# Two attention generators stepped at more ticks, a drain that becomes a poll, and a scale moved from VectorE to GpSimd

## Chip, cores and metric

The kernel runs on one core of one Trainium2 chip. The metric is device time in microseconds: 1560.05 us is the median of 3 runs (1555.44 to 1561.1). The profiled execution took 1560.56 us.

## What is computed

Two transformer blocks run one after the other on 512 tokens of width 1024, in float32. Each mixes tokens in several ways and ends in a feed-forward network. Cut to what matters here:

```python
def first_block(x, mem, ...):
    h = rmsnorm(x, g_pre_mix)
    cb, cc, cv, q, k, v, qm, ga, gb, gc = split(h @ w_in)
    y_a = (cb * causal_dwconv(cc * cv)) @ w_conv_out
    y_b = moba_attention(q, k, v, rel_bias) @ w_attn_out        # 8 heads of 64
    y_c = memory_attention(qm, rmsnorm(mem)) @ w_mem_out        # 4 heads of 128, 256 keys
    merged = sigmoid(ga) * y_a + sigmoid(gb) * y_b + sigmoid(gc) * y_c
    x = x + rmsnorm(merged @ w_out)
    u = causal_dwconv(rmsnorm(x) @ w_up)
    return x + rmsnorm((gelu(a) * g) @ w_down)                  # a, g = halves of u

def second_block(x, mem, ...):
    hq, hf, hi, hg, sq, sk, sv, iq, ik, iw, mq = split_in(rmsnorm(x) @ w_in)
    o_hg = hgrn2_mix(hq, hf, hi, hg)        # gated linear recurrence, chunks of 64
    o_sa = dsa_mix(sq, sk, sv, iq, ik, iw)  # attention on 128 keys picked by an index score
    o_mem = mem_mix(mq, rmsnorm(mem))       # 4 heads of 64, 256 keys
    x = x + concat(o_hg, o_sa, o_mem) @ w_out
    return x + (silu(a) * b) @ w_ffn_out    # a, b = halves of rmsnorm(x) @ w_ffn_in
```

## The kernel before

**GEMMs.** A float32 weight tile of 128 x 1024 is split into a high part (a cast on ScalarE, `wh`) and a low part (a subtraction on VectorE, `wl`), both in a 32-bit format that TensorE takes in one pass. A product is three passes: high by high, high by low, low by high (`passes`). Most jobs are 24 matmuls of 512 columns. Three pairs of buffers hold split tiles, and a tile is split two jobs ahead of its use.

**The order.** The program writes the order of every engine itself. `Program.job` lists the GEMM work. Beside it run generators, started by name with `Program.start`: each step of one issues some matmuls, reductions or copies of an attention head. After each few matmuls comes a tick. At a tick (`Program.tick`) each generator's credit grows by its rate, and one with a credit of 1 is advanced by a step, if the planner's `Clock` finds what it waits for ready (`clear`). Generators of rank 0 go first. `Program.drain(name)` closes a stage: it advances *all* generators until the named one has ended, and no GEMM is issued meanwhile.

**Block 1.** Convolution, then the gates: `gate(br, m, use)` is one job of 24 matmuls (`w_in_gate`, a tanh on ScalarE) and one of 12 (the branch's output weight). The generator `moba` runs the eight heads of local attention as four pairs (`moba_pair`, `causal_pair`): per pair four steps of scores with a reduction on VectorE (`tensor_tensor_reduce`) and an exponential on ScalarE, then row scalings on ScalarE, 20 transposes, copies out of PSUM, and 8 products. It is drained before the memory's queries are projected. `memT` norms and transposes the memory beside it. The generator `mem` runs the four heads of memory attention (`mem_heads`) beside the gates of the second branch and is drained before those of the third. `splits` splits block 2's weights ahead of time: a fetch on ScalarE's queue, a cast on ScalarE, a subtraction on VectorE, two writes on ScalarE's queue to DRAM, part after part. Its first twelve parts are drained after the third branch; then `w_out` follows.

**Block 2, the mixing stage.** `idx` makes the index scores and selects keys with VectorE (`top_keys`). `mem2` is memory attention, `fin_mq` (named `finm`) makes its queries. `hgrn_levels` computes the recurrence's products inside a chunk group by ten levels (m = 256 down to 0) for each half of the heads, two levels in flight. A level (`Level.steps`) is: subtractions on GpSimd, exponentials on ScalarE, a multiplication by the gated query (`scale`), and products on TensorE with a copy or a masked copy into an accumulator. `hgrn_tail(j)` makes the output of half j: products, a norm (ScalarE square, VectorE reduction, a power on GpSimd, VectorE multiplication) and 8 transposes. `sa` runs the selected attention as two pairs. The last GEMM, `w_out_2`, takes its first weight tile after `mem2`, the second after a drain of `sa`, the third after a drain of `tail0` and `tail1`.

In the rows that follow `p` is a PSUM bank, `s` a 128 x 1024 slot, `t` a scratch tile, `m` a column of statistics. All instructions carry line 96, that of the recording wrapper.

Of the kernel before, what the change touches and what calls it, by code (L numbers as in the profile page):

```python
# [13 lines left out]
ALU = mybir.AluOpType  # L14
# [187 lines left out]
def chain(*gens):  # L202
    def f():
        for g in gens:
            yield from g()
    return f


def body(tc, ctx, io):
    nc = tc.nc  # L210
    clock = Clock()
    v_, a_, g_, pe, sync = (Engine(e, n, clock) for e, n in (
        (nc.vector, "DVE"), (nc.scalar, "ACT"), (nc.gpsimd, "POOL"), (nc.tensor, "PE"), (nc.sync, "SP")))
# [27 lines left out]
    def passes(out, sh, sl, mh, ml, start, stop):  # L241
        mm(out, sh, mh, start=start, stop=False)
        mm(out, sh, ml, start=False, stop=False)
        mm(out, sl, mh, start=False, stop=stop)
# [50 lines left out]
    pr = Program(load, split, clock)  # L295
# [174 lines left out]
    def gemm_N(srcs, x, use, nt=NT):  # L470

        outs = []
        n = len(srcs)

        def f(kp):
            def g(w):
                if kp == 0:
                    outs.extend(bank() for _ in range(nt))
                if kp == n - 1:
                    for t in range(nt):  # L480
                        for kk in range(2):
                            tile_pass(outs[t], x(), 2 * kp + kk, t, w, kk, False, kk == 1)
                        use(t, outs[t])
                        if t < nt - 1:
                            yield
                    outs.clear()
                    return
                for kk in range(2):
                    i = 2 * kp + kk
                    for t in range(nt):  # L490
                        tile_pass(outs[t], x(), i, t, w, kk, i == 0, False)
                        if (kk * nt + t) % 2 and kk * nt + t < 2 * nt - 1:
                            yield
            return g
        for kp in range(n):
            pr.job(f(kp), [srcs[kp]])
# [128 lines left out]
    def toeplitz(hd):  # L625
        t = tmp()
        base = rdram[hd]
        for r in range(0, P, RB):
            a_.dma_start(t[r:r + RB, :], bass.AP(tensor=base.tensor, offset=base.offset + P - 1 - r, ap=[[639, RB], [1, 512]]))
        return t  # L630
# [20 lines left out]
    def stacked(out, q, kh, kl):  # L651
        mm(out, q, kh, start=True, stop=False)
        mm(out, q, kl, start=False, stop=True)
# [203 lines left out]
    def moba_pair(c):  # L857
        def g():
            while ("kl", c) not in qk:
                yield  # L860
            tz = [toeplitz(2 * c), toeplitz(2 * c + 1)]
            yield from causal_pair(
                lambda s: tuple(qk[n, c][:, s, :] for n in ("q", "kh", "kl")),
                lambda s, j: vN[j // 2][:, j % 2, (2 * c + s) * 64:(2 * c + s) * 64 + 64],
                lambda s, i: tz[s][:, 384 - P * i:512], lambda ps: oT.put(c, ps), extra=tz)
            yield
        return g
# [1 line left out]
    head_chunks([io["w_in_qk"][i] for i in (0, 4, 1, 5)], H, [use_q(0), use_k(0), use_q(1), use_k(1)],  # L869
                {(0, 1): small_consts, (0, 3): lambda: late_T(2), (1, 0): lambda: late_T(3), (1, 1): bias_rows})  # L870
    gemm_N([io["w_in_v"][j] for j in range(4)], H, use_v)
    pr.start("moba", chain(*(moba_pair(c) for c in range(4))), 0.35)
    cj = {c: conv_jobs(c) for c in range(4)}
    for c in range(4):
        for n, f in enumerate(cj[c]):
# [55 lines left out]
    def mem_head(hd):  # L931
        def g():
            def score(t, o):
                c = slice(t * P, (t + 1) * P)
                passes(o, qm.hi(hd)[:, c], qm.lo(hd)[:, c], mkv["kh"][:, hd, :], mkv["kl"][:, hd, :], True, True)
            yield from mem_heads([(score, lambda j: tuple(mkv[n][:, j, hd * P:(hd + 1) * P] for n in ("vh", "vl")), 0, P)],
                                 P ** -0.5, lambda ps: omT.put(hd, ps), parts=True,
                                 inputs=(qm.c[hd], mkv["kh"], mkv["kl"], mkv["vh"], mkv["vl"]))
        return g
# [10 lines left out]
    for c in range(4):  # L950
        chunk(io["w_mk"][c], lambda: memT, use_mk(c), cols=(0, 256))
    gemm_N([io["w_mv"][j] for j in range(4)], lambda: memT, use_mv, nt=2)
    pr.start("mem", chain(*(mem_head(hd) for hd in range(4))), 0.5)
    M = {n: [Parts(io[n][j]) for j in range(io[n].shape[0])]
         for n in ("w_hf", "w_hq", "w_iq", "w_mqsv", "w_sqk", "w_hi", "w_hg")}
    M["w_ikw"] = [Parts(io["w_ikw"])]
# [120 lines left out]
    def use_iq(c):  # L1077
        def f(ps):
            iq[c] = slot([P, 2, 512], F32R)
            stack_q([iq[c][:, s, :] for s in range(2)], ps)  # L1080
        return f
# [187 lines left out]

    def mem2_pair(c):  # L1270
        def g():
            hs = []
            for s in range(2):
                hd = 2 * c + s

                def score(t, o, hd=hd):
                    stacked(o, m2["q"].head(hd)[:, t * P:(t + 1) * P], m2["kh"].head(hd), m2["kl"].head(hd))
                hs.append((score, lambda j, hd=hd: m2["v"][:, j, hd * 64:(hd + 1) * 64], 64 * s, 64))
            yield from mem_heads(hs, 1.0, lambda ps: mixed.put(6 + c, ps),
                                 inputs=(m2["q"].head(2 * c), m2["q"].head(2 * c + 1), m2["kh"].all, m2["kl"].all))  # L1280
        return g
# [80 lines left out]
    class Level:  # L1362
# [39 lines left out]
                a_.activation(ke, ke, AF.Exp)  # L1402

        def scale(self):
            v_.tensor_tensor(out=self.qo, in0=self.qo, in1=self.blk(self.sq)[:, :, 1, :], op=ALU.mult)

        def steps(self):
            if self.m:
# [184 lines left out]
    def mixing():  # L1593
        next_head((late2, swap2), M["w_ikw"] + M["w_iq"][:3], [use_ikw, use_iq(0), use_iq(1), use_iq(2)], park)
        pr.start("idx", chain(sel0, index_weights, *(index_scores(c) for c in range(4)), top_keys(3),
                              top_keys(2), top_keys(1)))
        pr.start("hgrn", hgrn_levels)
        chunk(M["w_iq"][3], H, use_iq(3))
        gemm_N(M["w_mqsv"], H, use_mqsv)
        pr.start("finm", fin_mq, rank=0)  # L1600
        pr.ctl(load_kv2)
        for c in (0, 1):
            chunk(M["w_hf"][c], H, use_hf(c))
        for c in (0, 1):
            chunk(M["w_hq"][c], H, use_hq(c))
            if c == 0:
                pr.drain("finm")
                pr.start("mem2", chain(mem2_pair(0), mem2_pair(1)), rank=0)
        pr.start("gates0", gates(0), rank=0)
        gemm_N(M["w_sqk"], H, use_sqk)  # L1610
        pr.start("fin", fin_sqk, rank=0)
        for c in (2, 3):
            chunk(M["w_hf"][c], H, use_hf(c))
        for c in (2, 3):
            chunk(M["w_hq"][c], H, use_hq(c))
        pr.start("gates1", gates(1), rank=0)
        gemm_N(M["w_hi"], H, use_hi)
        pr.start("tail0", hgrn_tail(0))
        pr.start("sa", chain(sa_pair(0), sa_pair(1)))
        pr.start("tail1", hgrn_tail(1))  # L1620
        for c in range(4):
            chunk(M["w_hg"][c], H, use_hg(c))

    mixing()


# [175 lines left out]
```

## Time and profile before

| | us |
|---|---|
| median of 3 runs | 1560.05 |
| profiled execution | 1560.56 |
| its span, first to last instruction | 1558.7 |
| TensorE busy | 1511.8 (97%) |
| VectorE busy | 784.9 (50%) |
| ScalarE busy | 595.0 (38%) |
| GpSimd busy | 174.0 (11%) |

The profile is of one execution. Busy time of TensorE includes time at the lower clock level; a granted clock of 1.00 is 2.4 GHz and 0.50 is 1.2 GHz. In a timeline, a row's bracket is the engine's idle time before it and who released it. Releasers are inferred; where the engine named had long been done, it was another.

### The profile page before, as it was taken

The numbers are of one execution on the slowest core, as the hardware profiler recorded it, in microseconds if no ns is written. First come the engines' busy times: TensorE is split into PE (matmuls) and PEld (weight loads), VectorE is DVE, ScalarE is ACT, GpSimd is POOL, SyncE is SP. The second block draws the span as 40 slices with busy tenths as digits, with TensorE's granted clock in tenths as the row PEclk, the third lists the DMA queues.
The fourth block names the chain that finished last, engine by engine and source line by source line (L and its number), as shares of the span: only waits on it lengthen the run. The fifth ranks groups of instructions, "written<-read, shape, count | busy, mean of one in ns | idle before, by whom it ended". The sixth has DMA issues, their size and how long they took to land.

```text
span 1558.7 us, 20413 instructions
## 1 busy us (share of the span) xinstructions
PE 1511.8 (97%) x8059; PEld 1259.4 (81%) x8059; DVE 784.9 (50%) x1186; ACT 595.0 (38%) x1025; POOL 174.0 (11%) x290
## 2 busy tenths in 40 slices
PE   8999998998999999999999999999779999999999
PEld 7888887886888888888888888787568888888887
DVE  5355443465465676666522448885445333333231
ACT  5354354444453544434322334464524222222120
POOL 1000000022111100000000301442410000000000
PEclk9999999999999999999999999999779999999999
DMA  7412324255673274554655036442234312214200
GB/s 270 112 59 78 126 77 147 86 209 199 226 262 119 88 282 164 192 196 176 234 201 202 1 138 231 145 167 106 78 113 176 122 54 68 68 67 154 91 28 27
DMA packets 63622, 215.80 MB, mean 138 GB/s; under 512 B 7428, under 2 KB 7940, under 8 KB 63526
## 3 DMA queue, kind: packets, MB, share of 16 engines
q1 hardware_dynamic: 46512, 160.98, 29.1%
q10 hardware_dynamic: 17014, 53.52, 9.6%
q8 instruction: 63, 1.03, 0.3%
q14 instruction: 33, 0.27, 0.1%
HBM read 177.64 MB, written 36.83 MB: 138 GB/s over the span
## 4 chain that ended last, share of the span: by engine, by line
PE 93%; ACT 2%; DVE 2%; DMA 2%; issue 1%; POOL 1%; ACTq 0%; SPq 0%; DVEq 0%; POOLq 0%
PE p L96 93%; ACT s L96 2%; DVE s L96 1%; DMA s<-w_mqsv 1%; DMA s<-w_up 0%; POOL s L96 0%; POOL m L96 0%; DVE m L96 0%; DMA s<-x 0%; ACT t L96 0%; DVE wl L96 0%; ACT wh L96 0%; DVE t L96 0%; ACTq L96 0%; SPq L96 0%
## 5 line engine op out<-in xcount | busy, mean ns | idle before, releaser
L96 PE MATMUL p<-s,wh 128*128 128x512 f32 (+1 forms) x2480 | 760.1, 388 | 0.0
L96 PEld LDWEIGHTS p<-s,wh 128*128 128x128 f32 x2480 | 460.7, 188 | 92.6 <-issue 0.5
L96 PE MATMUL p<-s,wl 128*128 128x512 f32 (+1 forms) x1240 | 479.4, 387 | 0.0
L96 DVE TENSOR_TENSOR wl<-s,wh 128x1024 fp32r<-128x1024 f32 x209 | 246.9, 1184 | 301.7 <-ACT wh L96 295.2
L96 PE MATMUL p<-wh,s 128*128 128x512 f32 x1008 | 319.7, 392 | 0.6 <-ACT wh L96 0.6
L96 PE MATMUL p<-s,s 128*128 128x256 f32 (+6 forms) x2416 | 281.2, 295 | 18.3 <-DVE s L96 12.9
L96 ACT CAST wh<-s 128x1024 fp32r<-128x1024 f32 x209 | 207.7, 997 | 226.2 <-PE p L96 206.5
L96 PEld LDWEIGHTS p<-s,s 128*128 128x128 f32 (+2 forms) x2416 | 237.4, 169 | 57.6 <-issue 18.2
L96 PEld LDWEIGHTS p<-s,wl 128*128 128x128 f32 x1240 | 233.0, 188 | 47.2
L96 PEld LDWEIGHTS p<-wh,s 128*128 128x128 f32 x1008 | 190.5, 189 | 41.6 <-issue 1.2
L96 PE MATMUL p<-wl,s 128*128 128x512 f32 x504 | 197.4, 392 | 2.2 <-DVE wl L96 2.2
L96 DVE TENSOR_TENSOR s<-p,s 128x256 fp32r<-128x256 f32 (+3 forms) x144 | 75.9, 559 | 119.1 <-ACT s L96 68.6
L96 ACT ACTIVATE t<-p 128x512 f32<-128x512 f32 (+3 forms) x85 | 45.2, 553 | 180.3 <-PE p L96 178.8
L96 PEld LDWEIGHTS p<-wl,s 128*128 128x128 f32 x504 | 95.2, 189 | 21.3 <-DVE wl L96 2.5
L96 DVE TENSOR_TENSOR s<-s,s 128x1024 fp32r<-128x1024 f32 (+2 forms) x82 | 86.2, 1073 | 36.3 <-ACT s L96 36.3
L96 POOL TENSOR_SCALAR s<-t 128x512 fp32r<-128x512 f32 (+1 forms) x56 | 33.0, 589 | 613.5 <-DVE t L96 410.3
L96 ACT CAST s<-p 128x256 fp32r<-128x256 f32 (+2 forms) x120 | 50.5, 471 | 102.1 <-PE p L96 101.9
L96 PE MATMUL p<-ident,s 128*128 128x128 f32 x400 | 59.7, 293 | 19.9 <-DVE s L96 9.3
L96 DVE SCALAR_TENSOR_TENSOR t<-p,vecs,t 128x511 f32<-128x511 f32 x88 | 65.8, 748 | 24.6 <-ACT t L96 23.0
L96 ACT CAST s<-s 128x1024 fp32r<-128x1024 f32 (+1 forms) x64 | 61.8, 995 | 38.9 <-POOL s L96 28.1
L96 PEld LDWEIGHTS p<-ident,s 128*128 128x128 f32 x400 | 50.4, 151 | 30.3 <-DVE s L96 9.2
L96 ACT ACTIVATE s<-s,m 128x512 f32<-128x512 f32 (+3 forms) x96 | 49.2, 551 | 49.0 <-DVE m L96 49.0
(89 smaller groups left out, 711.5 us busy)
## 6 DMA issues: line engine op xcount, KB each, us to landing
wd<-s ACTq DMA_DIRECT2D x58, 512.0 KB, 3.3
s<-w_up SPq DMA_DIRECT2D x44, 512.0 KB, 4.5
s<-w_ffn_in SPq DMA_DIRECT2D x44, 512.0 KB, 3.3
wh<-wd SPq DMA_DIRECT2D x25, 512.0 KB, 3.5
wl<-wd SPq DMA_DIRECT2D x25, 512.0 KB, 4.4
s<-w_in_gate SPq DMA_DIRECT2D x24, 512.0 KB, 4.5
s<-w_down SPq DMA_DIRECT2D x22, 512.0 KB, 4.5
s<-w_ffn_out SPq DMA_DIRECT2D x22, 512.0 KB, 4.0
```

The costliest lines, as they stand in the source:

```text
L96: r = f(*args, **kw)
```

## The change

The rate of `moba` goes from 0.35 to 0.8 of a step per tick, that of `mem` from 0.5 to 1. In block 2 the drain of `finm` goes; the generator of memory attention polls for the end of `finm` at each tick instead. The multiplication of a level by the gated query is issued on GpSimd in place of VectorE (18 instructions). Nothing else is computed, and the instruction counts of TensorE and ScalarE stay as they are.

```diff
-    pr.start("moba", chain(*(moba_pair(c) for c in range(4))), 0.35)
+    pr.start("moba", chain(*(moba_pair(c) for c in range(4))), 0.8)
...
-    pr.start("mem", chain(*(mem_head(hd) for hd in range(4))), 0.5)
+    pr.start("mem", chain(*(mem_head(hd) for hd in range(4))))
...
     def mem2_pair(c):
         def g():
+            while "finm" in pr.bg:
+                yield
...
         def scale(self):
-            v_.tensor_tensor(out=self.qo, in0=self.qo, in1=self.blk(self.sq)[:, :, 1, :], op=ALU.mult)
+            g_.tensor_tensor(out=self.qo, in0=self.qo, in1=self.blk(self.sq)[:, :, 1, :], op=ALU.mult)
...
             if c == 0:
-                pr.drain("finm")
                 pr.start("mem2", chain(mem2_pair(0), mem2_pair(1)), rank=0)
```

The order of the instructions changes at three kinds of places.

TensorE at the drain of `moba`, before: the last scores of the fourth pair (`s_1011`, `s_1012` are its queries and keys) are followed at once by its transposes (`ident`).

```order
L96 MATMUL p_2115<-s_1011,s_975 128x256
L96 MATMUL p_2115<-s_1012,s_975 128x256
L96 MATMUL p_2118<-s_1011,s_975 128x256
L96 MATMUL p_2118<-s_1012,s_975 128x256
L96 MATMUL p_2126<-s_1011,s_975 128x128
L96 MATMUL p_2126<-s_1012,s_975 128x128
L96 MATMUL p_2129<-s_1011,s_975 128x128
L96 MATMUL p_2129<-s_1012,s_975 128x128
L96 MATMUL p_2146<-ident,s_2110 128x128
L96 MATMUL p_2146<-ident,s_2121 128x128
```

The same place now: the last gate's matmuls (`wh_2030`), eight transposes of the memory (`s_1953`), then those of the fourth pair.

```order
L96 MATMUL p_2118<-s_1482,wh_2030 128x512 x2
L96 MATMUL p_2118<-s_1482,wl_2031 128x512
L96 MATMUL p_2132<-ident,s_1953 128x128 x4
L96 MATMUL p_2139<-ident,s_1953 128x128 x4
L96 MATMUL p_2146<-ident,s_1924 128x128
L96 MATMUL p_2146<-ident,s_2007 128x128
```

All the scores of the fourth pair moved ahead of the drain, among the gates. At the drain of `mem` eight transposes and six matmuls stood on TensorE between the second and the third branch; now none does, and the third branch follows directly.

ScalarE at the drain of `splits`, before: one part (`s_3830`, fetched beside the last gate) is cast and written, then the third and fourth tiles of `w_out` are cast (`wh_3851`, `wh_3885`).

```order
L96 ACTIVATE t_3815<-p_3787,hbg 128x512
L96 CAST wh_3817<-s_3709 128x1024
L96 DMA s_3830<-w_hq 128x1024
L96 CAST s_3841<-s_2010 128x512
L96 CAST s_3844<-s_3830 128x1024
L96 DMA wd_3848<-s_3844 128x1024
L96 DMA wd_3848<-s_3845 128x1024
L96 CAST wh_3851<-s_3746 128x1024
L96 CAST wh_3885<-s_3785 128x1024
```

The same place now: a part of `w_hf` and then, fetched only after its writes, one of `w_hq`.

```order
L96 ACTIVATE t_3806<-p_3778,hbg 128x512
L96 CAST wh_3808<-s_3700 128x1024
L96 DMA s_3821<-w_hf 128x1024
L96 CAST s_3832<-s_2049 128x512
L96 CAST s_3835<-s_3821 128x1024
L96 DMA wd_3839<-s_3835 128x1024
L96 DMA wd_3839<-s_3836 128x1024
L96 DMA s_3842<-w_hq 128x1024
L96 CAST s_3844<-s_3842 128x1024
L96 DMA wd_3848<-s_3844 128x1024
L96 DMA wd_3848<-s_3845 128x1024
L96 CAST wh_3851<-s_3737 128x1024
```

A fetch, a cast and two writes now stand in front of `wh_3851` that stood earlier before.

GpSimd in the levels of the second half of the heads, before (`s_8603` and `s_8497` are the cumulated gates, the third size is the level): only subtractions.

```order
L96 TENSOR_TENSOR s_7383<-s_8603,s_8497 128x8x64
L96 TENSOR_TENSOR s_7382<-s_8603 128x16x32
L96 TENSOR_TENSOR s_7381<-s_8603,s_8497 128x16x32
L96 TENSOR_TENSOR s_7384<-s_8603 128x32x16
L96 TENSOR_TENSOR s_7383<-s_8603,s_8497 128x32x16
L96 TENSOR_TENSOR s_7382<-s_8603 128x64x8
L96 TENSOR_TENSOR s_7381<-s_8603,s_8497 128x64x8
```

The same levels now: the scales (by `s_8406`, the gated query) stand in pairs between the subtractions of the level pairs.

```order
L96 TENSOR_TENSOR s_7383<-s_8595,s_8495 128x8x64
L96 TENSOR_TENSOR s_7382<-s_8595 128x16x32
L96 TENSOR_TENSOR s_7381<-s_8595,s_8495 128x16x32
L96 TENSOR_TENSOR s_7384<-s_7384,s_8406 128x8x64
L96 TENSOR_TENSOR s_7382<-s_7382,s_8406 128x16x32
L96 TENSOR_TENSOR s_7384<-s_8595 128x32x16
L96 TENSOR_TENSOR s_7383<-s_8595,s_8495 128x32x16
L96 TENSOR_TENSOR s_7382<-s_8595 128x64x8
L96 TENSOR_TENSOR s_7381<-s_8595,s_8495 128x64x8
L96 TENSOR_TENSOR s_7384<-s_7384,s_8406 128x32x16
L96 TENSOR_TENSOR s_7382<-s_7382,s_8406 128x64x8
```

The scales left VectorE's list, and a level's subtractions now stand behind the scales of the pair ahead. In the first half the levels come earlier against the GEMMs: the products and transposes of `tail0` stand on TensorE before the end of the first `w_out_2` tile, and the transposes of the first `sa` pair after it.

## Rows read from the trace of the kernel before

**Rows 1.** The page, part 1: busy time, share, instructions of each engine.

```profile
PE 1511.8 (97%) x8059; PEld 1259.4 (81%) x8059; DVE 784.9 (50%) x1186; ACT 595.0 (38%) x1025; POOL 174.0 (11%) x290
```

**Rows 2.** TensorE's timeline: start, us, operation, count, [idle before it and releaser].

```profile
240.45 2.64 PE L96 MATMUL p<-s,s 128*128 128x512 f32 x16
...
248.44 4.53 PE L96 MATMUL p<-ident,s 128*128 128x128 f32 x20 [5.35 <-ACT s L96]
252.90 2.42 PE L96 MATMUL p<-s,s 128*64 128x512 f32 x16
255.25 0.73 PE L96 MATMUL p<-s,wh 128*128 128x512 f32 x2
```

**Rows 3.** Windows: stretch, us, busy by engine (count), granted clock, DMA share, GB/s.

```profile
248.00:250.00 2.00, 1.56 (x8) 1.56 (x9) 0.00 (x0) 2.00 (x6) 0.00 (x0) 0.50 0.00 0
...
560.00:600.00 40.00, 40.00 (x178) 33.12 (x177) 26.87 (x33) 17.40 (x21) 2.48 (x4) 1.00 0.59 223
```

**Rows 4.** TensorE's timeline at the drain of `mem`.

```profile
380.28 2.12 PE L96 MATMUL p<-ident,s 128*128 128x128 f32 x8 [2.64 <-POOL s L96]
385.02 0.80 PE L96 MATMUL p<-s,s 128*128 128x512 f32 x1 [2.62 <-ACT s L96]
...
388.69 1.03 PE L96 MATMUL p<-s,wh 128*128 128x512 f32 x2
```

**Rows 5.** ScalarE's timeline at the drain of `splits` (ACTq: DMAs that it issues).

```profile
458.57 1.58 ACT L96 CAST s<-s 128x512 fp32r<-128x512 f32 x2 [3.26 <-POOL s L96]
460.18 1.59 ACTq L96 DMA_DIRECT2D wd<-s  x2
461.80 2.00 ACT L96 CAST wh<-s 128x1024 fp32r<-128x1024 f32 x2 [1.66 <-PE p L96]
```

**Rows 6.** TensorE's timeline, then VectorE's, at the start of `w_out`.

```profile
456.21 0.39 PE L96 MATMUL p<-wh,s 128*128 128x512 f32 x1
...
462.89 2.36 DVE L96 TENSOR_TENSOR wl<-s,wh 128x1024 fp32r<-128x1024 f32 x2 [1.48 <-ACT wh L96]
```

**Rows 7.** The tile view of `w_hq`, four fetches by `splits`.

```profile
DMA to landing us min/median/max: 3.3/3.5/3.6
```

**Rows 8.** ScalarE's timeline inside the drain of `mem`.

```profile
375.98 0.70 ACTq L96 DMA_DIRECT2D s<-w_mqsv  x1
...
383.44 1.04 ACT L96 CAST s<-s 128x1024 fp32r<-128x1024 f32 x1 [6.33 <-DMA s<-w_mqsv]
```

**Rows 9.** TensorE's timeline in the drains that end the mixing stage.

```profile
1092.53 0.39 PE L96 MATMUL p<-wh,s 128*128 128x512 f32 x1
...
1127.61 0.50 PE L96 MATMUL p<-wh,s 128*128 128x512 f32 x1
...
1143.61 6.04 PE L96 MATMUL p<-s,s 128*128 128x128 f32 x36 [1.28 <-POOL s L96]
...
1155.91 0.78 PE L96 MATMUL p<-wh,s 128*128 128x512 f32 x1
```

**Rows 10.** VectorE's timeline in the same drains (CUSTOM_DVE_ANT_0 is the score reduction).

```profile
1097.31 0.69 DVE L96 TENSOR_TENSOR s<-p,m 128x512 f32<-128x512 f32 x1 [1.69 <-POOL m L96]
1097.92 0.68 DVE L96 CUSTOM_DVE_ANT_0 s<-p,s 128x512 f32<-128x512 f32 x1
...
1130.44 5.83 DVE L96 TENSOR_TENSOR s<-s,s 128x1024 fp32r<-128x1024 f32 x6
```

**Rows 11.** ScalarE's timeline in the same drains.

```profile
1111.80 3.71 ACT L96 ACTIVATE s<-s,m 128x512 f32<-128x512 f32 x8
...
1129.16 3.90 ACT L96 CAST s<-s 128x1024 fp32r<-128x1024 f32 x4
1132.96 2.27 ACT L96 ACTIVATE s<-s 128x512 f32<-128x512 f32 x4
```

**Rows 12.** GpSimd by tile (ns min/median/max), then VectorE by form (busy, mean ns).

```profile
L96 POOL TENSOR_TENSOR s<-s,s x14: 1053/1152/1727, 1018.7 to 1126.6; 128x512 f32<-128x512 f32 x14
...
L96 DVE TENSOR_TENSOR s<-s,s 128x512 f32<-128x512 f32 x18 | 12.8, 727 | 1.9 <-ACT s L96 1.9
```

## Prediction

> **What bounds the kernel now.** I read the page's engine line first: TensorE is busy for 1511.8 of 1558.7 us [rows 1]. The lists of the order hold 6,705 TensorE rows before and after, so the change can win back only the 47 us in which TensorE stands idle, and what runs at the lower of its two clock levels. Next I read the windows: where nothing disturbs it, TensorE runs 178 matmuls in 40 us at granted clock 1.00 [rows 3], 0.225 us each. That is my unit for cover: a job of 24 matmuls hides 5.4 us.
>
> Then I looked in TensorE's timeline for rows with an idle time in brackets. Three places carry most of it, and the change touches all three. Place A is the drain of block 1's local attention. Its 16 score passes start at 240.45, its transposes only at 248.44, after 5.35 us of waiting for ScalarE, and the next projection at 255.25 [rows 2]. Place B is the drain of block 1's memory attention: waits of 2.64 us for GpSimd and 2.62 us for ScalarE, and the next projection at 388.69 [rows 4]. Place C is the end of the mixing stage, where block 2's attention and its levels are drained: from 1092.53 to 1155.91 TensorE has two weight tiles and fragments [rows 9].
>
> A wait costs more than itself. After the 5.35 us gap of place A the granted clock of 248 to 250 us is 0.50, the 1.2 GHz level [rows 3]. So its 20 transposes, 4.53 us [rows 2], would take 2.3 at the 2.4 GHz level. I add 2.3 us to a gap of that length; that is an estimate from this one place.
>
> **The change part by part.**
>
> *Rate 0.35 to 0.8 (place A).* Before, the whole fourth pair stands in the drain: 14.8 us from 240.45 to 255.25. Its work at the higher level is 2.64 + 2.3 + 2.42 = 7.4 [rows 2], so 7.4 us are lost. After, its scores, exponentials and row scalings stand among gate matmuls, and the scalings precede the last gate's tanh, so TensorE has what its transposes need. Eight transposes of the memory's norm now stand ahead of them; these were hidden before and are equal work. The last copies out of PSUM run on ScalarE and VectorE while the transposes go on. I take the whole 7.4; a remaining wait of up to 3 us gives the lower bound, 4.4. The denser steps meet no less GEMM overall; I cost them at nothing, under the convolution and gate matmuls. If that cover fails it is one of the small waits in the range.
>
> *Rate 0.5 to 1.0 (place B).* The waits start 2.64 before 380.28, so at 377.64; the next projection comes at 388.69 [rows 4]: 11.05 us. The work is eight transposes (8/20 of 2.3 = 0.9) and six 512-column matmuls (6 x 0.225 = 1.4). After, none of it stands in the drain. Gain 11.05 - 2.3 = 8.7; lower bound 6, if the denser heads wait once under the gates.
>
> *What B's drain also did.* The loop of a drain advances every other generator. Before, it pushed the splitting of block 2's weights on by a part, out of step with TensorE: ScalarE issues a fetch at 375.98 and waits 6.33 us for it, until 383.44 [rows 8]. Without that loop the splits reach their own drain one part later, so that drain holds a whole extra fetch, cast and two writes on ScalarE ahead of the weight casts of `w_out`. This is a loss. Before: the split's cast follows the cast that opens the pair of 458.57, so it starts near 459.1; ScalarE issues its writes until 461.77, casts the third `w_out` tile at 461.80 [rows 5], and VectorE's low part of that tile, first of a pair that begins at 462.89, ends half of 2.36 later, at 464.1 [rows 6]. TensorE starts `w_out` at 456.21 [rows 6] and has two tiles ready, 48 x 0.225 = 10.8 us, so it needs the third at 467.0: 2.9 to spare. After: the next fetch is issued at about 461.8, and once it has landed the same chain follows, 464.1 - 459.1 = 5.0 us. Landings of such a fetch lie between 3.3 us [rows 7] and 383.44 - 375.98 = 7.5 [rows 8]; the queues are busy here with 1 MB of the previous part's writes, so I take 5.4. Then the tile is ready at 461.8 + 5.4 + 5.0 = 472.2, a wait of 5.2, and a fall of the clock: 5.2 + 2.3 = 7.5 us lost. The bounds are 461.8 + 3.3 + 5.0 - 467.0 = 3.1 without a fall and 7.3 + 2.3 = 9.6.
>
> *`finm`.* Memory attention of block 2 now polls instead of a drain; TensorE has no waiting row there before, so nothing is won, and no instruction stands behind a hardware wait that wasn't there. Zero, with rank and rate equal.
>
> *Scale on GpSimd (place C).* 18 multiplications leave VectorE, 0.727 us each, 13.1 in all [rows 12]. The nearest GpSimd row, the same form and shape, takes 1.152 in the median and 1.053 to 1.727 [rows 12], so a level's own chain grows by 0.4, at most 1.0 us. VectorE's queue matters more: before, a scale stood in it behind whatever waited. In the first half the shorter queue brings the levels forward, so that the outputs of heads 0 and 1 stand ahead of the first drain instead of inside it.
>
> The sum of place C, in three stretches of the attention drain. (1) From its start, 1092.53, to pair 1's first reduction, 1097.92 [rows 9, 10]: 5.4 us before. After, pair 0's 20 transposes (2.3), its products (2.4) and pair 1's scores (four passes, 0.9) come first, with copies between: 8.3. (2) From there to ScalarE's last row scaling, 1111.80 + 3.71 [rows 11]: 17.6 before. After, the output stage's normalisation, where VectorE stood 1.69 us for GpSimd [rows 10], is out of the way; I count 12.7. (3) To the next weight tile, 1127.61 [rows 9]: 12.1 before, with two levels' products in it; after, these stand ahead of the transposes: 6.5. Together 35.1 becomes 27.5, a gain of 7.6. The tile before the drain gains 2 more: work worth 2.3 + 2.4 leaves it and some 2 enters. Then the second drain, 1127.61 to 1155.91, 28.3 us: before, the exponentials of levels 4 and 2 start at 1132.96, behind four weight casts of 3.90 us [rows 11], and their scales end a VectorE row of six operations and 5.83 us whose first four are the low parts [rows 10]. After, both stand ahead, and one level less is left. Only the last level's exponential waits for the casts: casts until 5.5 us after the tile starts, exponential 0.6, GpSimd 1.2, two products and their masks 2.5, the copies 1.6, then the output stage's 1155.91 - 1143.61 = 12.3 [rows 9]: 23.7, a gain of 4.6. Place C: 7.6 + 2 + 4.6 = 14. Bounds: 0, if GpSimd's order eats it, and 17.
>
> The Trainium skill, GPSIMD Engine Reference, section "Key points", calls VectorE "structurally ~2× faster" for elementwise work and says that GpSimd contends with VectorE instructions of two SBUF inputs, as this scale is. The trace gives a ratio of 1.152 / 0.727 = 1.6, with single rows of 1.727. By the page each scale would cost twice 0.727, 1.45 us, and the sum would move by nine times 0.3, under 3 us; both are estimates.
>
> **Sum.** The profiled execution took 1560.56 us, 1.9 outside the span, and lies 0.5 above the median of 1560.05. 1560.6 - 7.4 - 8.7 + 7.5 - 14 = 1538.0.
>
> **The rivals.** (a) *The end of mixing keeps its length.* GpSimd works in order: a scale waits for ScalarE's exponential, and the next level's subtractions stand behind it. Nine levels, each with 0.4 more for the scale and about 1.1 for the blocked queue, give 14 us back: 1552. For it: GpSimd gets 18 x 1.152 = 21 us more in a stage that ends on its chains. Against it: in the new order the scales of two levels stand side by side, and the subtractions of the next ones between. (b) *The splits cost nothing,* because the fetch lands early and TensorE is late itself: 1538.0 - 7.5 = 1530.5. Against it: even 3.3 us is too long by 3.1. (c) *The first drain still waits,* since it still holds the fourth pair's transposes, so the change of rate does half of what it says: 1538 + 5 = 1543. (d) *Slower: GpSimd becomes the bound of the whole mixing stage.* If its operations take 1.7, the largest seen [rows 12], and slow VectorE's beside them, the first nine levels lose their cover of GEMM too: each product then waits some 2.2 us, 9 x 2.2 = 20 on top of (a): 1572. It decides where GpSimd's work in the first half, some 45 operations, outgrows the 60 us of GEMM around it. Against it: the median is 1.152.
>
> **How the numbers follow.** The forecast has 50%, its own range 1531 to 1546; (a) 20%, (b) 12%, (c) 10%, (d) 8%. The time is the forecast's, 1538. The range 1530 to 1553 leaves out (d), half of (b) and a tail of (a). A measurement of this kernel tells a difference from none at about 0.5%, so 1552.2 is the line: the forecast, (b), (c) and half of (a) are faster, 82%; the rest of (a) and a little of (d) are the same, 11%; slower is 7%.
>
> **What the next profile would show.** No TensorE wait of over 3 us near 235 to 250 (the fourth pair's transposes right behind the memory's) and none near 365 to 385. A new wait about 11 us after `w_out` starts, near 450 us, of some 5 us behind ScalarE's cast of a weight tile, with a second fetch of `w_hq` just ahead, and clock 0.5 after it. From the end of the first `w_out_2` tile to the start of the third some 51 us instead of 63, and 18 more GpSimd multiplications of 1.1 to 1.3 us. The forecast falls if GpSimd's scales show waits with TensorE behind them, if the splits' wait exceeds 8 us, or if TensorE waits among the first 200 us.

## The result: 1541.55 us, 1.1% faster

Over four runs each the median went from 1558.97 us to 1541.55 us (1539.41 to 1542.65). The ratio is 0.9889, 95% interval 0.9872 to 0.9906, so 14.7 to 20.0 us. The forecast was 1538, in a range of 1530 to 1553. The profiled execution took 1542.65 us, its span is 1540.9, 17.9 less than before.

The page of the kernel after, part 1, against [rows 1]: TensorE is busy 4.7 us less, so most of the gain is idle time, and VectorE has given work to GpSimd.

```profile
PE 1507.1 (98%) x8059; PEld 1256.6 (82%) x8059; DVE 772.3 (50%) x1168; ACT 594.6 (39%) x1025; POOL 198.2 (13%) x308
```

**Place A.** TensorE's timeline of the kernel after, at the drain of `moba`: start, length, operation, count. Where [rows 2] has 5.35 us of waiting and slow transposes, 28 transposes (eight of them the memory's) follow the last gate without a wait. The granted clock stays 1.00, as the window over the place shows (last row, third figure from the end).

```profile
243.06 3.22 PE L96 MATMUL p<-ident,s 128*128 128x128 f32 x28
246.20 3.62 PE L96 MATMUL p<-s,s 128*64 128x512 f32 x16
249.75 0.73 PE L96 MATMUL p<-s,wh 128*128 128x512 f32 x2
...
240.00:280.00 40.00, 39.91 (x225) 33.26 (x224) 17.78 (x24) 15.91 (x24) 0.00 (x0) 1.00 0.42 145
```

**Place B.** The window over the stretch where `mem` was drained: TensorE is busy throughout, at full clock. The waits of [rows 4] are gone.

```profile
360.00:392.00 32.00, 32.00 (x147) 26.56 (x147) 15.35 (x17) 12.03 (x17) 6.36 (x9) 1.00 0.68 230
```

**The splits.** ScalarE's timeline at their drain, to be held against [rows 5]: a second fetch of `w_hq` is issued at 446.97, 5.59 us after `w_out` began (441.38); its cast starts 5.47 us later, and the casts of the third and fourth `w_out` tiles stand behind it.

```profile
446.97 0.71 ACTq L96 DMA_DIRECT2D s<-w_hq  x1
452.44 1.04 ACT L96 CAST s<-s 128x1024 fp32r<-128x1024 f32 x1 [7.12 <-DMA s<-w_hq]
453.51 1.59 ACTq L96 DMA_DIRECT2D wd<-s  x2
455.14 1.99 ACT L96 CAST wh<-s 128x1024 fp32r<-128x1024 f32 x2 [1.66 <-DVE s L96]
```

TensorE waits for the high part of that tile, then for the low part:

```profile
456.24 0.80 PE L96 MATMUL p<-wh,s 128*128 128x512 f32 x1 [3.82 <-ACT wh L96]
457.50 0.80 PE L96 MATMUL p<-wl,s 128*128 128x512 f32 x1 [0.46 <-DVE wl L96]
```

The windows behind it show what the wait leaves: the lower clock level (the granted clock is the third figure from the end).

```profile
456.00:460.00 4.00, 3.30 (x7) 2.31 (x8) 3.78 (x4) 4.00 (x6) 0.00 (x0) 0.50 0.54 216
460.00:462.00 2.00, 2.00 (x6) 1.52 (x6) 2.00 (x3) 0.92 (x1) 0.00 (x0) 0.50 0.88 215
```

**Place C.** TensorE's timeline in the two drains of `w_out_2`, against [rows 9]. The last matmul of the first tile starts at 1084.59, the second tile at 1113.43, the third at 1139.47. Three waits for GpSimd's scales and copies remain, and two for VectorE's `t`, which is the output stage's normalisation.

```profile
1086.33 0.44 PE L96 MATMUL p<-ident,s 128*128 128x128 f32 x2 [0.48 <-DVE t L96]
1088.46 3.11 PE L96 MATMUL p<-s,s 128*128 128x256 f32 x16 [1.69 <-DVE t L96]
...
1104.73 2.31 PE L96 MATMUL p<-s,s 128*32 128x32 f32 x128 [4.13 <-POOL s L96]
...
1113.43 0.50 PE L96 MATMUL p<-wh,s 128*128 128x512 f32 x1
...
1123.13 2.47 PE L96 MATMUL p<-s,s 128*32 128x32 f32 x132 [2.34 <-POOL s L96]
1126.86 6.36 PE L96 MATMUL p<-s,s 128*128 128x128 f32 x36 [1.26 <-POOL s L96]
...
1139.47 0.78 PE L96 MATMUL p<-wh,s 128*128 128x512 f32 x1
```

TensorE's waits over the whole execution, by releaser (us in total, times, longest): those for VectorE's slots before, then after the change, and those for GpSimd's slots after it (3.9 us before).

```profile
PE p L96 <- DVE s L96: 22.2, 14, 2.9
...
PE p L96 <- DVE s L96: 8.4, 6, 2.5
PE p L96 <- POOL s L96: 7.7, 3, 4.1
```

### The profile page after: what moved, and what is told of

Read it like the earlier page. It is cut to its first block, busy times and chain, and to the rows that moved or that the text cites. A ratio compares the mean times of both kernels' runs of the same rounds, so it can differ in the third digit from the quotient of the medians.

```text
span 1540.9 us, 20410 instructions
## 1 busy us (share of the span) xinstructions
PE 1507.1 (98%) x8059; PEld 1256.6 (82%) x8059; DVE 772.3 (50%) x1168; ACT 594.6 (39%) x1025; POOL 198.2 (13%) x308
## 4 chain that ended last, share of the span: by engine, by line
PE 94%; DVE 2%; ACT 1%; POOL 1%; issue 1%; DMA 1%; SPq 0%; ACTq 0%; DVEq 0%; POOLq 0%
PE p L96 94%; ACT s L96 1%; DVE s L96 1%; POOL s L96 1%; POOL m L96 1%; DVE wl L96 0%; DMA s<-x 0%; DMA s<-w_hq 0%; ACT wh L96 0%; ACT t L96 0%; DVE m L96 0%; DVE t L96 0%; SPq L96 0%; ACTq L96 0%; DVEq L96 0%
## 5 line engine op out<-in xcount | busy, mean ns | idle before, releaser
L96 PE MATMUL p<-s,s 128*128 128x256 f32 (+6 forms) x2416 | 277.1, 289 | 11.6 <-POOL s L96 7.7
L96 PEld LDWEIGHTS p<-s,s 128*128 128x128 f32 (+2 forms) x2416 | 235.0, 164 | 49.4 <-issue 11.8
L96 DVE TENSOR_TENSOR s<-s,s 128x1024 fp32r<-128x1024 f32 (+1 forms) x64 | 73.3, 1167 | 37.8 <-ACT s L96 37.8
L96 DVE SCALAR_TENSOR_TENSOR t<-p,vecs,t 128x511 f32<-128x511 f32 x88 | 65.8, 748 | 24.6 <-ACT t L96 23.0
L96 ACT ACTIVATE t<-p,vecs 128x512 f32<-128x512 f32 x44 | 34.3, 780 | 88.0 <-PE p L96 87.9
```

The costliest lines, as they stand in the source:

```text
L96: r = f(*args, **kw)
```

## One table for all kernels

The matmuls on weight tiles (those with `wh` or `wl`) come in the same sequence in every kernel here. I number them from 0 in each trace and take the time from the start of one to the start of another, so that each place has its own length. A: 0 to 768, which ends at the projection behind the drain of `moba`. B: 768 to 1584, the start of `w_out`. S: 1584 to 1705, over the drain of `splits` and the norm behind `w_out`, to block 1's feed-forward network. N: from there 55 of them further. M: to the last one of the first `w_out_2` tile. D1 and D2: from there to the second tile, and on to the third. E: the third tile and what follows, to the first weight tile of the last feed-forward network. From there every kernel takes 315.32 to the last of these matmuls and 341.07 to 341.09 to the end of its span. "First" is the start of matmul 0.

| kernel | first | A | B | S | N | M | D1 | D2 | E |
|---|---|---|---|---|---|---|---|---|---|
| before | 42.30 | 212.95 | 200.96 | 54.15 | 25.89 | 556.27 | 35.08 | 28.30 | 61.74 |
| before again (e9) | 41.05 | 212.90 | 200.36 | 54.15 | 28.66 | 556.24 | 33.76 | 26.73 | 60.42 |
| after | 43.16 | 206.60 | 191.62 | 61.52 | 27.48 | 554.21 | 28.84 | 26.04 | 60.31 |
| e1 `moba` alone | 41.10 | 206.60 | 199.88 | 54.18 | 25.89 | 556.39 | 35.12 | 28.32 | 61.71 |
| e10 the same again | 41.52 | 206.60 | 199.89 | 54.14 | 25.87 | 556.29 | 35.06 | 28.30 | 61.73 |
| e2 `mem` alone | 39.68 | 212.53 | 191.55 | 61.43 | 27.49 | 556.31 | 35.05 | 28.31 | 61.72 |
| e3 scale alone | 39.84 | 212.88 | 200.35 | 54.18 | 28.66 | 552.69 | 29.96 | 23.98 | 60.32 |
| e4 after, splits at rate 1 | 41.79 | 206.61 | 191.62 | 54.18 | 27.48 | 553.60 | 28.40 | 23.97 | 61.88 |
| e5 e4 without the scale | 39.55 | 206.59 | 191.60 | 54.18 | 27.49 | 556.38 | 35.26 | 28.07 | 61.55 |
| e6 order alone | 41.81 | 206.60 | 191.51 | 61.44 | 27.49 | 559.04 | 31.10 | 26.16 | 61.71 |
| e7 engine alone | 40.88 | 213.03 | 200.43 | 54.15 | 28.73 | 554.86 | 32.04 | 30.17 | 60.26 |
| e8 scale twice | 42.44 | 206.60 | 191.60 | 61.44 | 27.50 | 557.74 | 32.69 | 26.69 | 61.56 |
| e11 m = 1 on VectorE | 40.24 | 206.59 | 191.60 | 54.15 | 27.41 | 554.86 | 29.88 | 24.18 | 61.77 |
| e12 the same, booked | 42.63 | 206.59 | 191.62 | 54.16 | 25.90 | 553.16 | 28.47 | 24.17 | 61.73 |

After minus before: first +0.86, A -6.35, B -9.34, S +7.37, N +1.59, and M, D1, D2, E together -11.99. The sum is -17.86, the difference of the spans 17.87. N and E hold no edit: TensorE runs the same sequence there in every kernel, and yet E is either 60.3 to 60.4 or 61.6 to 61.9, with the old order (e9, e7) as with the new (after, e3).

## Experiments

**e1 and e10: the first edit alone.**

```diff
-    pr.start("moba", chain(*(moba_pair(c) for c in range(4))), 0.35)
+    pr.start("moba", chain(*(moba_pair(c) for c in range(4))), 0.8)
```

> The kernel before with one edit, the rate of block 1's local attention 0.35 to 0.8. Theory: the fourth pair leaves the drain, so the 5.35 us wait at 243.09 to 248.44 and the half clock behind it go; the traces of before and after put this at 6.4 us (the next projection comes 5.5 us earlier although the steady chain began 0.85 us later). Median near 1552.6, 6 to 7 us under the kernel before in the same call. Rival (c): a wait of 3 us or more stays in the drain, gain 3 us or less. Rival: the gain is given back later, where a later wait is set by a transfer and not by TensorE: gain 0 to 2.

Measured: 1555.88 us, ratio 0.9977 (0.9962 to 0.9991) to the kernel before, a gain of 1.4 to 5.9 us. The trace has A at 206.60, to the hundredth what it is after the full change: the mechanism is there, without rest, and nothing in S gives it back. But the median gains less than the 6.35. So it was run again, for a second profile.

> The kernel before with the rate of the local attention 0.8, once more, since its median gain of 3.6 us is less than the 6.4 us that the first trace shows at place A. If place A gives 6.3 again, counted from the first weight tile to the projection behind the drain, the gain there is real and the rest of the difference is elsewhere in the execution (start, 495 to 515 us, end of mixing). If place A gives about 3.6 here, the wait or its clock differs between executions.

A is 206.60 again. The two profiled executions took 1552.07 and 1552.29 us, 3.6 to 3.8 under the median of this kernel. Both had a mean granted clock of 0.987; eight of the ten executions behind the median had 0.984 or 0.985. So the clock differed, but at which of the other places the two traces don't show, and that stays open.

**e2: the second edit alone.**

```diff
-    pr.start("mem", chain(*(mem_head(hd) for hd in range(4))), 0.5)
+    pr.start("mem", chain(*(mem_head(hd) for hd in range(4))))
```

> The kernel before with one edit, the rate of block 1's memory attention 0.5 to 1.0. Theory: the drain of memory attention gives back 9.3 us and the drain of the weight splits takes 7.4 of it, since its last part is fetched one step later: median 1.9 us under the kernel before, near 1557, with a wait of 3 to 5 us for ScalarE's cast before the third tile of w_out. Rival (b) in a new form: the wait at the splits hangs on TensorE's earlier arrival through the first edit and not on the missing loop of the drain; then this kernel gains 7 to 9 us, 1550 to 1552.

Measured: 1559.45 us, ratio 0.9999 (0.9986 to 1.0012). In the table B is 9.41 us shorter and S takes 7.28 back. TensorE's timeline shows the same wait as after the full change, though TensorE gets there later:

```profile
458.52 0.80 PE L96 MATMUL p<-wh,s 128*128 128x512 f32 x1 [3.73 <-ACT wh L96]
```

So the wait belongs to this edit, which takes the loop of the drain of `mem` away from the splits, and does not need the earlier arrival that the first edit brings. By itself this edit is worth nothing that the medians show (the interval is 2.2 us faster to 1.9 us slower).

**e3: the scale alone.** The one line of `scale` from `v_` to `g_` in the kernel before.

> The kernel before with one edit, the scale of the HGRN levels on GpSimd. Theory: the end of the mixing stage is shortened by this edit alone, by the 9.0 us read from the two traces (start of the first w_out_2 tile to start of the third): 9 us under the kernel before, near 1550. From the end of the first w_out_2 tile to the start of the third some 54.7 us as after the full change, 63.4 before. Rival (a): GpSimd's order gives it back, 0 to 2 us. Rival: the gain at the end of mixing needs the poll or the earlier arrival of block 2, 2 to 5 us.

Measured: 1546.06 us, ratio 0.9917 (0.9899 to 0.9934), a gain of 10.3 to 15.8, more than the 9 expected: M to E are 14.4 us shorter in its trace. By the ratios the three edits alone give 3.6 + 0.2 + 12.9 = 16.7 us, the whole change 17.3. They add up within their intervals; the poll has no share that could be seen. The expected 9 was read from two timelines as if the lead of 7.5 us at the start of the feed-forward network had lasted until the mixing stage; the table shows that 1.6 of it went in N before that. The 1.4 us of E, behind the third tile, weren't counted either.

**e4: splits at every tick.**

```diff
-    pr.start("splits", splits(0, 12), 0.5)
+    pr.start("splits", splits(0, 12), 1.0)
```

> The changed kernel with one more edit, the weight splits stepped at every tick (rate 0.5 to 1.0), so that the fetch of their last part is issued one weight cast ahead of the drain. Theory: the wait before the third w_out tile and the half clock behind it go, 7.4 us: median near 1534, 7 us under the changed kernel. Rival: the denser splits load ScalarE and the DMA queues under the gates, so that new waits of TensorE stand there and the time stays at 1540 or more. Rival: the fetch still lands late (an issue one cast earlier is worth only 1 to 2 us of the 5.4 us landing), gain 1 to 3 us.

Measured: 1531.75 us (1530.74 to 1535.01), ratio 0.9829 (0.9808 to 0.9850) to the kernel before, and 9.8 us under the changed kernel's median. ScalarE's timeline: the last part is fetched at 437.51, with a weight cast and the drain's first casts between it and its own cast (the second of the pair at 442.38).

```profile
437.51 0.34 ACTq L96 DMA_DIRECT2D s<-w_hq  x1
438.08 1.04 ACT L96 CAST wh<-s 128x1024 fp32r<-128x1024 f32 x1
442.38 1.57 ACT L96 CAST s<-s 128x512 fp32r<-128x512 f32 x2 [3.26 <-POOL s L96]
443.98 1.59 ACTq L96 DMA_DIRECT2D wd<-s  x2
445.61 2.00 ACT L96 CAST wh<-s 128x1024 fp32r<-128x1024 f32 x2 [1.66 <-PE p L96]
```

S is back at 54.18: the wait was the fetch alone, and the denser splits cost nothing under the gates (A and B as after). Of the 9.8 us, S is 7.3. In the two traces the rest is mostly the start (1.4) and D2 (2.1), with E 1.6 the other way, and this edit touches none of them. This is a kernel better than both.

**e5: e4 with the scale back on VectorE.**

> The kernel with the weight splits at every tick, with one part undone: the scale of the HGRN levels is back on VectorE. Theory: places A and B and the mended splits stay, the end of mixing goes back to the kernel before. By the offsets read so far the scale was worth 13.3 us there: median near 1545, and from the end of the first w_out_2 tile to the start of the third some 63.4 us instead of 52.4. Rival: the order that the earlier stages leave behind helps the end of mixing too, so that undoing the scale costs 6 us or less, 1538.

Measured: 1546.31 us, ratio 0.9909 (0.9885 to 0.9933). From the end of the first `w_out_2` tile to the third 63.33, as in the kernel before. The earlier stages help the end of mixing in nothing. This kernel has the poll, too: its M to E, 681.26, is that of the kernels with the drain of `finm` and the old order (681.38 to 681.54 in before, e1, e2 and e10), with the same sequence on TensorE.

**e6 and e7: is it the order or the engine?** The planner lets a generator step only where its clocks for VectorE and ScalarE are not late; GpSimd's clock isn't asked:

```python
    def clear(self, names):
        late = self.now + self.LEAD
        return (self.t["DVE"] <= late and self.t["ACT"] <= late
```

So the edit does two things: it moves 18 operations, and it takes them off the account that holds steps back. A wrapper that issues on one engine and books on the other parts the two (e6 in the changed kernel, e7 in the kernel before):

```diff
+    x_ = Engine(nc.vector, "POOL", clock)     # e7: Engine(nc.gpsimd, "DVE", clock)
...
-            g_.tensor_tensor(out=self.qo, in0=self.qo, in1=self.blk(self.sq)[:, :, 1, :], op=ALU.mult)
+            x_.tensor_tensor(out=self.qo, in0=self.qo, in1=self.blk(self.sq)[:, :, 1, :], op=ALU.mult)
```

> The changed kernel with its own order of instructions on every engine, but the 18 scales issued on VectorE, at the same places among the others; the planner still books them on GpSimd. Theory O (the order gives the gain: the planner waits for VectorE and ScalarE, not for GpSimd, so booking the scales there lets it bring levels and outputs forward): the end of mixing stays as short as after the change, within 2 us, 1540 to 1543. Rival E (the engine gives it: a scale on VectorE stands behind what waits there and holds up what follows): most of the 12 us are lost, 1549 to 1553.

Measured: 1550.37 us, ratio 0.9940 (0.9917 to 0.9962): 8.8 us over the changed kernel. TensorE's waits, by releaser: the 8.4 us for VectorE's slots after the change are 21.5 here.

```profile
PE p L96 <- DVE s L96: 21.5, 14, 3.8
```

Four of them stand among the GEMMs already, before the drains, where the changed kernel has none: 4.8 us, as much as M is longer. The waits from 1000 to 1087 us, and two of the rows:

```profile
PE p L96 <- DVE s L96: 4.8, 4, 1.8
```

```profile
1030.82 1.74 PE L96 MATMUL p<-s,s 128*64 128x64 f32 x48 [1.76 <-DVE s L96]
...
1056.83 0.75 PE L96 MATMUL p<-s,s 128*32 128x32 f32 x64 [1.71 <-DVE s L96]
```

> The kernel before with its own order on every engine, but the 18 scales issued on GpSimd; the planner still books them on VectorE. Theory O (the order gives the gain): the end of mixing stays at 63 us from the end of the first w_out_2 tile to the start of the third, or loses a little to the slower engine: 1558 to 1562. Rival E (the engine gives it): 12 to 14 us are gained without any change of order, 1546 to 1548.

Measured: 1558.00 us, ratio 0.9990 (0.9975 to 1.0006): no gain. With the old order the levels are still in the drains, and TensorE waits for GpSimd instead:

```profile
PE p L96 <- POOL s L96: 13.6, 6, 3.8
```

Neither theory holds alone. In the traces the order without the engine has 678.01 us in M to E and the engine without the order 677.33, against 681.39 before and 669.40 after; but the second profile of the unchanged kernel has 677.15 (e9), so these 3.4 and 4.1 us are no evidence of a gain. Nor do the medians show one: the 8.1 us that e6 gains are what A, B and S give in its trace (8.5), and e7 gains nothing. The gain needs both: the planner brings the levels forward, and VectorE's queue is then short enough to let them run there.

**e8: every scale twice.** A second multiplication on GpSimd, into a tile that nothing reads, ahead of each; all other orders unchanged.

> The changed kernel with every scale done twice on GpSimd, the first time into a tile that nothing reads; order of all else unchanged. 18 operations of 1.06 to 1.7 us more, 20 to 23 us of GpSimd. Theory: GpSimd's chain ends last only in the two drains (the waits of 4.1 and 2.3 us behind its scales): two scales more in the first, one in the second, 3 to 5 us with what the clock loses: 1544 to 1547. Rival (d): GpSimd is near the bound in the whole stage; then most of the 20 us show, 1556 to 1562, with new waits of TensorE for GpSimd between 1000 and 1080 us.

Measured: 1550.98 us, ratio 0.9942 (0.9920 to 0.9964), 9.4 us over the changed kernel. The 18 operations take 25.0 us of GpSimd (the first row below, by form), so about four tenths show, twice what was expected and half of what the rival said. M is 3.5 longer, D1 3.85. TensorE's waits for GpSimd's slots grow from 7.7 us in 3 to 17.1 in 10, by as much as is lost. Four of them, 3.8 us, stand in M, where the changed kernel has none, and the first drain has new ones of 1.43 and 1.48 us. So GpSimd was not the bound, but its slack under the GEMMs is less than one operation per level. The second block has the waits in M (total, times, longest), the longest of them, and the last one of the first drain.

```profile
L1409 POOL TENSOR_TENSOR twice<-s,s 128x512 f32<-128x512 f32 x18 | 25.0, 1391 | 4.6 <-ACT s L96 4.6
```

```profile
PE p L96 <- POOL s L96: 3.8, 4, 1.5
...
1045.98 0.76 PE L96 MATMUL p<-s,s 128*32 128x32 f32 x64 [1.55 <-POOL s L96]
...
1112.45 1.08 PE L96 MATMUL p<-s,s 128*32 128x32 f32 x64 [1.48 <-POOL s L96]
```

**e9: the kernel before, profiled again.**

> The kernel before once more, unchanged, for a second profile of it. One thing to read: which of its losses differ from one execution to the next. Expected the same at places A and B (half clock behind both waits) and at the splits; different, if the clock falls only now and then there, in the stretch from 495 to 515 us, where the first profile kept 1.00 and those of five other kernels fell for 3.4 to 6.8 us, and in the start (up to 3 us).

One execution, 1557.14 us. A, B, S and M come out within 0.6 us of the first profile, D1 to E are 4.2 us shorter with the same instructions in the same order, and N is 2.8 longer. The windows say why: busy time is equal (62.9 us), the granted clock is not. First the kernel before, then its second profile:

```profile
1075.00:1160.00 85.00, 62.97 (x831) 50.17 (x830) 38.15 (x72) 37.90 (x76) 27.79 (x45) 0.80 0.28 99
495.00:515.00 20.00, 17.26 (x79) 13.85 (x78) 15.03 (x24) 9.35 (x22) 4.30 (x11) 1.00 0.72 263
```

```profile
1075.00:1160.00 85.00, 62.93 (x846) 50.63 (x845) 39.03 (x72) 37.90 (x76) 27.83 (x45) 0.86 0.28 100
495.00:515.00 20.00, 17.26 (x68) 13.54 (x67) 13.14 (x20) 8.22 (x18) 3.72 (x10) 0.83 0.72 263
```

**e11 and e12: the last scale back on VectorE,** on top of e4. In the second drain the scale of the level of 1 takes 1.65 us on GpSimd, and VectorE's four low parts were taken for the reason. e11 issues the scales of that level on VectorE and keeps the order; e12 books them there too.

```diff
-            g_.tensor_tensor(out=self.qo, ...)
+            (x_ if self.m == 1 else g_).tensor_tensor(out=self.qo, ...)     # e12: v_ in place of x_
```

> The changed kernel with the splits at every tick, its order kept, and only the scales of the level of 1 issued on VectorE. Theory (the last scale is slow, 1.65 us, because VectorE's low parts run beside it): on VectorE it starts when they end, some 0.2 us later, and takes 0.7, so TensorE's wait of 2.4 us before the level's products falls to 1.6 to 1.8; median within 1.5 us of 1531.75. Rival: the scale now stands behind VectorE's masks too and the wait grows to 3 us or more; 1533 to 1535.

Measured: 1534.86 us, ratio 0.9838 (0.9812 to 0.9863); e4 has 1531.75. VectorE's timeline in the second drain: the scale stands behind the masked copies, so it starts 0.8 us after the low parts have ended.

```profile
1107.55 5.47 DVE L96 TENSOR_TENSOR s<-s,s 128x1024 fp32r<-128x1024 f32 x4
1112.94 0.97 DVE L96 COPY_PREDICATED t<-lmask,p 128x256 f32<-128x256 uint32 x2
1113.81 0.69 DVE L96 TENSOR_TENSOR s<-s,s 128x512 f32<-128x512 f32 x1
```

TensorE's wait there is 2.58 us, against 2.36 in e4: the rival's mechanism is there, but it is 0.2 of the 3.1 us. Most of the loss is in M (+1.26) and D1 (+1.48), which neither theory named. The theory's premise was wrong, too. In e4 the low parts end at 1111.96, 0.3 us after the scale starts, and in e7 the same scale takes 1.48 us in a stretch in which VectorE is idle (GpSimd's row, then VectorE's next one):

```profile
1135.77 1.48 POOL L96 TENSOR_TENSOR s<-s,s 128x512 f32<-128x512 f32 x1 [0.76 <-ACT s L96]
...
1138.46 0.45 DVE L96 COPY_PREDICATED t<-lmask,p 128x256 f32<-128x256 uint32 x1 [3.15 <-PE p L96]
```

> The same as the run before, but the planner also books these scales on VectorE, so that the order may change. Theory (what the planner books on VectorE sets how early it brings steps forward): with 2 of 18 scales back on VectorE's account the order changes near the last levels of the first half and at the end; the end of mixing loses 0 to 4 us against the same kernel with all scales booked on GpSimd, 1531 to 1535. Rival: booking is without effect, the time is that of the run before within 1 us.

Measured: 1531.99 us, ratio 0.9817 (0.9796 to 0.9838), the time of e4, with an order that differs near the end of the levels. M to E are 667.53 against 667.87. The booking has an effect, then: it takes back what e11 lost, but there is nothing beyond that.

## Why the prediction held, step by step

**Place A: 7.4 predicted, 6.35 measured.** The wait and the half clock went entirely, as the step said, and none of the denser steps shows anywhere. The term is 1.05 too large: I put the last 16 products at 2.42 and said that the copies would run beside the transposes; they take 3.62 in the row of 246.20, at full clock. They read copies of the transposes just before, so short waits for these are likely, but the profile lists none, and they aren't shown. The bounds, 4.4 to 7.4, held it.

**Place B: 8.7 predicted, 9.3 measured between the two profiles.** The waits went entirely. Kernels with the old order have 199.88 to 200.96 in B, those with the new one 191.51 to 191.62, so the gain is 8.3 to 9.4 by the execution, and 8.7 lies within.

**The splits: +7.5 predicted, +7.37 measured.** The landing was taken as 5.4 and was 5.47; the wait as 5.2 before the clock, and the tile's low part came at 457.4 where TensorE needed it at 452.2. This is the step that few would look for: the loss sits 70 us behind the edit that makes it. e2 shows that it belongs to that edit, e4 that it is the fetch alone. Rival (b), splits at no cost, fell.

**`finm`: zero predicted.** No kernel tried it alone, but the three other edits alone add up to the whole within their intervals, and e5, with the poll and the old scale, has the M to E of the kernel before to 0.3 us.

**Place C: 14 predicted, 12.0 between the two profiles, and 14.4 and 13.5 in e3 and e4.** This is the term that was mis-sized in the profile of the changed kernel, and e9 shows that neither profile alone sizes it: the order of the kernel before takes 681.3 to 681.5 us in M to E in five profiles and 677.15 in one; the new order takes 669.40, 666.95 and 667.87. Against the second profile of the kernel before the gain would be 7.8, and 1.4 of the 12.0 is E, which no edit moved. So how near 12.0 comes to 14 is in part luck of the two executions; the medians give 10.3 to 15.8 for the scale alone (e3). The prediction gave the gain to VectorE's shorter queue and to the levels that it brings forward; e6 and e7 show that both are needed. In parts, after against the prediction: the tile before the drain gains 2.06 (2); the first drain is 28.84 (27.5); the second 26.04 (23.7), but 23.98 and 23.97 in e3 and e4, where the 36 products of the output stage take 4.29 us at a granted clock of 1.00, in place of the 6.36 above at 0.66. Inside the first drain stretch (1) was short: 11.8 us to the first reduction (1096.37) in place of 8.3, since TensorE waits 0.48 and 1.69 us for the output stage's normalisation. VectorE's and GpSimd's timelines of the kernel after show it held up by a low part of 2.35 us, beside two GpSimd multiplications; alone, it takes 1.23.

```profile
1083.27 2.35 DVE L96 TENSOR_TENSOR wl<-s,wh 128x1024 fp32r<-128x1024 f32 x1
...
1115.11 1.23 DVE L96 TENSOR_TENSOR wl<-s,wh 128x1024 fp32r<-128x1024 f32 x1 [0.25 <-ACT wh L96]
```

```profile
1081.99 2.54 POOL L96 TENSOR_TENSOR s<-s,s 128x512 f32<-128x512 f32 x2
...
1118.65 1.99 POOL L96 TENSOR_TENSOR s<-s 128x512 f32<-128x512 f32 x1 [4.86 <-PE p L96]
1121.43 1.64 POOL L96 TENSOR_TENSOR s<-s,s 128x512 f32<-128x512 f32 x1 [0.79 <-ACT s L96]
```

Stretch (2), 12.7, was 12.1, and stretch (3), 6.5, was 4.9.

**The price of a scale.** The tile view after the change gives GpSimd's operations of this form as min/median/max in ns; before, the median was 1152 [rows 12]. Read one by one, the 18 scales take 24.6 us: thirteen 1.27 to 1.30, the levels of 2 and 1 1.51 to 1.64, and one 1.72. The prediction's 1.152 was the median of other operations of this form, and 18 of them would be 20.7; the price was 0.2 us per scale too small.

```profile
L96 POOL TENSOR_TENSOR s<-s,s x34: 1060/1288/1722, 980.2 to 1121.4; 128x512 f32<-128x512 f32 x34
```

Against VectorE's 0.727 that is 1.8 in the median. The Trainium skill, GPSIMD Engine Reference, section "Key points", says about 2 for elementwise work, and contention of GpSimd with VectorE instructions of two SBUF inputs: the first is near, the second agrees with the low part of 2.35 us and the subtraction of 1.99. The measured numbers decide.

**A sign of being wrong that did appear.** The prediction said that it falls if GpSimd's scales show waits with TensorE behind them. Two do: the waits of 4.13 and 2.34 us at place C (rows of 1104.73 and 1123.13) end when scales end. The time came in all the same: in the same two drains the kernel before had four such waits behind VectorE's scales (2.88, 1.38, 2.47 and 2.08 us, 8.8 together), and now it is two, 6.5 together. The sign was put too widely. Waits for GpSimd among the GEMMs would have told of rival (d), and only e8 has them.

**The rivals.** (a), GpSimd's order eats place C: fell, place C is shorter by more than the profiles of one kernel differ, and the scale alone gains 10.3 us at least (e3); the rival was nearer than it looks, since one more operation per level costs 9.4 us (e8). (c), the first drain still waits: fell, A has none. (d), GpSimd bounds the whole stage: fell for the same reason as (a); in the changed kernel no wait for GpSimd stands in M.

**What the sum left out.** N lost 1.59 us and the start 0.86, and both belong to no edit. N is 25.9, 27.4 to 27.5 or 28.7 in kernels with the same instructions there, in four, seven and three of the fourteen traces. The predicted 22.6 us of gain against the measured 17.9 of the spans is A 1.05 too large, C 2.0, N 1.6 and the start 0.9, with 0.8 the other way in B and the splits.

## What to carry to other kernels

A drain that advances every generator is a hidden scheduler: who empties it must ask which others it used to push forward, and where they will stand now. A move to another engine is worth its place in the order: the same 18 operations gained nothing in the old order, and the new order lost most of its gain with them on the old engine. When one edit gains at one place and loses elsewhere, the loss may need one small number more (here the rate of the splits: 7.3 us in S, 9.8 in the medians).

## What was not expected of the hardware

The same wait costs different times in different executions. Behind block 1's `w_out`, TensorE waits for the feed-forward network's first tile; the idle times before its two rows are 0.55 to 0.58 and 2.18 to 2.20 us in all fourteen traces. The granted clock of 495 to 515 us was 1.00 in the first profile of the kernel before and 0.83 in the second, and N with it 25.89 or 28.66. In the drains, too, the clock made 2.1 us of difference in D2 between kernels of one order there (26.04 after, 23.97 in e4, with granted clocks of 0.66 and 1.00 over the 36 products). Differences of 2 to 4 us between two single profiles are therefore no evidence of an edit here; the places A, B and S, which repeat to 0.2 us in the order of the changed kernel, are.
